# Hybrid attention layer on one core: value projection of two head pairs per product

## The chip, the cores and the metric

The kernel runs on 1 core of one Trainium2 chip. The time is device microseconds of one execution; runs are compared by their median. Three runs of the kernel before took 1176.5, 1177.23 and 1177.47 us, median 1177.23.

## The reference

One decoder layer on x (1 x 2048 x 1024, f32). A modulated RMS norm gives h, and one product gives all inputs of two attention branches:

```python
mod = jax.nn.silu(c) @ w_ada[l] + b_ada[l]
h = rms_norm(x, g_pre[l]) * (1.0 + scale[:, None, :]) + shift[:, None, :]
proj = h @ w_in[l]
qa, ka, va, fa, za, qb, kb, vb, zb = jnp.split(proj, split_points, axis=-1)
oa = forgetting_attention(qa, ka, va, fa + b_fgate[l]) * jax.nn.silu(za)     # 8 heads of 64, causal
ob = sliding_window_sink_attention(rope(qb), rope(kb), vb, sinks[l]) * jax.nn.silu(zb)   # 8 heads, window 128
y = jnp.concatenate([oa, ob], axis=-1) @ w_out[l]
x = x + gate[:, None, :] * rms_norm(y, g_post[l])
```

(Reshapes are left out.) The change concerns va = h @ w_in[:, 1024:1536], the values of the eight heads of the first ("fox") branch, and the order in which va and the gates zb of the second ("sliding window") branch are computed.

## The kernel before, in words

**Numbers in two parts.** To reach f32 accuracy with f16 products each matrix is kept as a high and a low f16 part, and a product is three matmuls: high x high, low x high, high x low. hT holds h transposed, in four chunks ("ci") of 512 positions, with 8 slices of the model dimension (KT = 8).

**Weights.** A weight tile of 128 columns goes through eight steps, each hung on a place of the work list: `w_load` (L211, a DMA issued by POOL into a raw tile, pool `wpool`, two buffers shared by all keys), `w_max` (L220, DVE), a round trip through DRAM (`w_back`), `w_scale` (L233, a chain of small DVE instructions), `w_high` (L251, one ACT instruction of 128 x 1024 at L256), two `w_low` (L259, DVE, L262) and `w_done`. The split parts are a tile tagged `whl`; it comes from `wpq` (one buffer) for keys that begin with q or k, else from `wpool` (two buffers). With one buffer, `w_high` of the next key waits until TensorE has read the last of the key before.

**The work list.** `punits` is a list of "units", each a piece of a projection that takes TensorE some 0.65 us: for z, q and k three matmuls of 512 columns (`proj_units`, L339), for the values twelve matmuls of 128 columns (`value_units`, L346 to L372, matmul at L357). A group of eight units holds one of three PSUM banks (`bk`), then ACT copies it out (L362), DVE makes the low part (L366, two instructions) and the bank is released. `add` (L940) appends units and hangs the weight steps on unit numbers ahead of the first use ("lead": load 42 units ahead, high 9 ahead). `after(n, f)` and `tick()` delay ACT and DVE pieces by ticks. Every engine executes its own instructions in the order in which this program emits them.

**The stages.** Up to unit 144 (some 148 us) h is built. Then, until unit 440 (some 416 us), 32 "windows" of sliding-window attention (`Pair`) are interleaved with units, about nine units to a window. A window on TensorE is `pv` (L924, 24 matmuls, tile pob), `turn` (L900, four transposes, tile pxb) and `scores` (L871, twelve matmuls, tile pss), some 2 us in all. Behind it come ACT `fold` (L905), DVE `fold` (L906), four POOL selects (L910, L912) that make `ptb`, which the next window's `pv` reads; and DVE `maxima` (L879 to L886, ends with `b_nb`), then four ACT exponentials (L893, tile sm_), which the next window's `turn` reads. So two chains run from one window to the next, one through ACT, DVE and POOL, one through DVE and ACT. After unit 440 come the first query/key projections and the rest of the values, then fox attention (scores from 477 to 1010 us), with the output projection from 975 us on.

**Order of groups before.** zb0, zb1, va0, zb2, zb3, va1, va2 among the windows (in the list at L962), va3 half before and half after the projection qk0 (L1026, L1060). Each va key is one pair of heads: 128 columns, four chunks of eight units.

**Scratch.** In the fox stage's last head and in the output stage a pool `stpo` (L1377) of four buffers of 2 KB per partition serves as raw storage of w_out and as scratch.

Of the kernel before, what the change touches and what calls it, by code (L numbers as in the profile page):

```python
# [10 lines left out]
F32 = mybir.dt.float32  # L11
F16 = mybir.dt.float16
BF16 = mybir.dt.bfloat16
# [22 lines left out]
XM, XR, VW = 66, 69, 129  # L36
# [7 lines left out]
def hybrid_layer(  # L44
# [17 lines left out]
    V, A, G, PE, SP = nc.vector, nc.scalar, nc.gpsimd, nc.tensor, nc.sync  # L62
# [64 lines left out]
    right = ExitStack()  # L127
# [16 lines left out]
    hT = [(hpool if i < 2 else hlate).tile([P, 2, KT, CH], F16, name=f"hT{i}") for i in range(NCH)]  # L144
# [33 lines left out]
    bk = [ps_bk.tile([P, CH], F32, name=f"bk{n}") for n in range(3)]  # L178
    held, order_ = set(), [0, 1, 2]

    def bank(hold=False):
        n = next(n for n in order_ if n not in held)
        order_.remove(n)
        order_.append(n)
        if hold:
            held.add(n)
        return n

    def release(n):
        held.discard(n)  # L190
        order_.remove(n)
        order_.append(n)
# [14 lines left out]
    wq = {}  # L207
# [43 lines left out]
    def w_high(key):  # L251
        raw, pw, sw = wq[key]
        width = VB if key == "vb" else P
        pool = vbw if key == "vb" else wpq if key[0] in "qk" else wpool
        whl = pool.tile([P, 2, KT, width], F16, tag="whl", name=f"wh_{key}")
        A.activation(whl[:, 0], raw[:], AF.Identity, scale=sw[:])  # L256
        wq[key].append(whl)

# [13 lines left out]
    def o_store(on, pool, ci, rows_, cols_, eng, lag):  # L272
# [11 lines left out]
        after(lag, lambda: A.activation(oh[:, :, 0], on, AF.Copy))  # L284
        after(lag + 1, low)

    pws = {}
    scl, isc, czs, kaps, nscl, snd = {}, {}, {}, {}, {}, {}

# [40 lines left out]
    def proj_units(key, ci, evac):  # L330

        st_ = {}

        def unit(k):
            if k == 0:
                st_[0] = bank(True)
            whl, ps = wq[key], bk[st_[0]][:]
            for n, (a, b) in enumerate(((0, 0), (0, 1), (1, 0))):
                PE.matmul(ps, whl[:, a, k, :], hT[ci][:, b, k, :],  # L339
                          start=(k == 0 and n == 0), stop=(k == KT - 1 and n == 2))  # L340
            if k == KT - 1:
                evac(ps, lambda: release(st_[0]))

        return [lambda k=k: unit(k) for k in range(KT)]

    def value_units(key, ci, dst):  # L346

        st_ = {}

        def unit(n_):  # L350
            if n_ == 0:
                st_[0] = bank(True)
            whl, ps = wq[key], bk[st_[0]][:]
            u = n_ // 2
            for k in range(4 * (n_ % 2), 4 * (n_ % 2) + 4):
                for n, (a, b) in enumerate(((0, 0), (1, 0), (0, 1))):
                    PE.matmul(ps[:, u * P:(u + 1) * P], hT[ci][:, a, k, u * P:(u + 1) * P], whl[:, b, k, :],  # L357
                              start=(k == 0 and n == 0), stop=(k == KT - 1 and n == 2))
            if n_ == 7:
                hi, lo = dst()  # L360
                pv4 = ps.rearrange("p (t h d) -> p t h d", t=4, h=2)
                after(1, lambda: A.activation(hi, pv4, AF.Copy, scale=PS_SCALE))  # L362

                def low():
                    for h in range(2):
                        V.scalar_tensor_tensor(lo[:, :, h], pv4[:, :, h], PS_SCALE, hi[:, :, h],  # L366
                                               op0=ALU.mult, op1=ALU.subtract)
                    release(st_[0])

                after(2, low)  # L370

        return [lambda n=n: unit(n) for n in range(8)]  # L372

    def evac_z(kt, key, ci):
        def evac(ps, free):
            t = op_.tile([P, CH], F32, tag="tz", name="tz")

            def mul():
                V.scalar_tensor_tensor(t[:], t[:], 1.0, ps, op0=ALU.add, op1=ALU.mult)
                free()  # L380
# [69 lines left out]
    start = ExitStack()  # L450
# [223 lines left out]
    fx, abp = {}, None  # L674

    def open_fox():
        nonlocal abp
        xlx.close()
        abp = swa_pool("abp", 4)
        early.close()  # L680
        fxv = right.enter_context(tc.tile_pool(name="fxv", bufs=1, side="right", reuse_waits="tile"))
        vt = fx["vt"] = fxv.tile([P, NB, 8, VW], F16, name="vt")
        fx["lk"] = fxv.tile([P, LW], F16, name="lk")
        fx["lq"] = [fxv.tile([P, LW], F16, name=f"lq{n}") for n in range(2)]
        fx["cst"] = cst = fxv.tile([P, XR], F16, name="cst")
# [12 lines left out]
    def va_units(j, ci):  # L698
        rows_ = slice(4 * ci, 4 * ci + 4)
        heads = slice(2 * j, 2 * j + 2)  # L700
        return value_units(f"va{j}", ci, lambda: (fx["vt"][:, rows_, heads, 0:64], fx["vt"][:, rows_, heads, 65:VW]))


    swa = ExitStack()

# [5 lines left out]
    stp = swa_pool("stp", 2)  # L711
# [7 lines left out]
    vb = kvp.tile([P, NB, 2, P], F16, name="vb")  # L719
# [218 lines left out]
    pkeys, punits = [], []  # L938

    def add(key, us):  # L940
        if key not in pkeys and key not in ("kb", "vb"):
# [24 lines left out]

    def at_slice(n, f):
        events.setdefault(n, []).append(f)
# [205 lines left out]
    foxl, foxo = ExitStack(), ExitStack()  # L1174
# [196 lines left out]
    def open_out():  # L1371
        nonlocal op_, stp
        foxl.close()
        hpx.close()
        wo = foxo.enter_context(tc.tile_pool(name="wo", bufs=1, reuse_waits="tile"))
        op_ = foxo.enter_context(tc.tile_pool(name="opo", bufs=2, reuse_waits="tile"))
        stp = foxo.enter_context(tc.tile_pool(name="stpo", bufs=4, reuse_waits="tile"))  # L1377
        oio["w"] = wo.tile([P, 2, KT, D], F16, name="wohl")

        fm = sm(1, "w_p2")  # L1380
        V.tensor_reduce(fm[:], fac8[:], axis=AX.X, op=ALU.max)
        V.reciprocal(fm[:], fm[:])
        V.tensor_tensor(ysc[:], wrt[:], fm[:], op=ALU.mult)
        V.tensor_scalar(wsc[:], fac8[:], ysc[:], None, op0=ALU.mult)
# [19 lines left out]
        V.scalar_tensor_tensor(w_slot(8 + k)[:, cc], raw[:], wsc[:, k:k + 1], hi, op0=ALU.mult, op1=ALU.subtract)  # L1404

    oio = {}

    class Out:

# [319 lines left out]
```

## Time and profile before

| what | us |
|---|---|
| median of 3 runs | 1177.23 |
| profiled execution | 1173.47 |
| its span, first to last instruction | 1171.7 |
| TensorE busy in the span | 1126.7 |
| VectorE (DVE) busy | 924.3 |
| ScalarE (ACT) busy | 661.7 |
| value matmuls of va (L357), busy, 1536 instructions | 91.9 |

The profiled execution is one run, with the hardware profiler on; 1.8 us of its time lie outside the span. "PE" is the matmul side of TensorE, "PEld" its weight loads, which overlap. In a row of a timeline the first number is the start in us from the start of the span, the second the time until the last of the merged instructions ended; in square brackets stands the idle time of the engine before it and what ended that. A matmul's shown duration holds its latency in the pipeline, so the pace of a stream of matmuls is read from start to start.

### The profile page before, as it was taken

To read this page: it belongs to the slowest core of one execution; us is meant where nothing else is said; L and a number is where in the kernel's file an instruction comes from. 1 tells how busy PE (TensorE), PEld (TensorE's weight loads), DVE (VectorE), ACT (ScalarE), POOL (GpSimd) and SP (SyncE) were. 2 spreads that over 40 slices of the span, in tenths; PEclk is the share of its full clock that TensorE was granted. 3 is DMA by queue.
4 is the path that set the end of the run, shared out by engine and by line. 5 is a ranking of instruction groups with operands and counts; after the bars stand their busy time and mean duration, and the time that the engine had idled before them with its cause. 6 is when DMAs were issued, how large, how long until landed. Compare 5 with 4: busy or idle time off the path is not lost.

```text
span 1171.7 us, 26770 instructions
## 1 busy us (share of the span) xinstructions
PE 1126.7 (96%) x10637; PEld 671.1 (57%) x10637; DVE 924.3 (79%) x2167; ACT 661.7 (56%) x1150; POOL 182.4 (16%) x293
## 2 busy tenths in 40 slices
PE   5899999999999999999999999999999999999997
PEld 2476555765558876555555555555556555544444
DVE  7876668677776548788888999888897897778885
ACT  2784445454555421476666767666676788633332
POOL 1000125535454421010000100001000000000000
PEclk9899999999999999999999999999999999999999
DMA  9745333314324323423424332222311237677742
GB/s 333 259 142 88 82 94 78 91 52 108 95 70 95 48 60 74 67 56 86 74 71 65 106 55 58 61 49 67 52 37 43 72 88 226 138 216 200 193 144 108
DMA packets 123481, 120.19 MB, mean 103 GB/s; under 512 B 64948, under 2 KB 100828, under 8 KB 123356
## 3 DMA queue, kind: packets, MB, share of 16 engines
q1 hardware_dynamic: 112088, 85.69, 27.1%
q0 software_dynamic: 10832, 32.50, 13.0%
q8 instruction: 83, 1.36, 0.6%
q14 instruction: 42, 0.34, 0.2%
q10 hardware_dynamic: 436, 0.28, 0.1%
HBM read 64.75 MB, written 25.18 MB: 77 GB/s over the span
## 4 chain that ended last, share of the span: by engine, by line
PE 74%; DVE 13%; DMA 7%; ACT 3%; issue 2%; SPq 1%; POOL 0%; DVEq 0%; ACTq 0%; POOLq 0%
PE bk L339 27%; PE bk L1522 13%; PE bk L357 7%; PE sta L1311 4%; PE sta L1310 4%; PE bk L1261 4%; PE poa L1336 3%; PE poa L1337 3%; PE poa L1334 3%; DMA wa<-in_w_ada_dram 2%; DVE a_m L1264 2%; PE pss L871 1%; PE pob L924 1%; DVE pha L1324 1%; PE pxb L900 1%
## 5 line engine op out<-in xcount | busy, mean ns | idle before, releaser
L1317 ACT ACTIVATE p<-sta,lift,scl_qk 128x1024 f32<-128x1024 f32 (+2 forms) x160 | 171.9, 1075 | 131.1 <-PE sta L1311 80.4
L339 PE MATMUL bk<-hT,wh_qk 128*128 128x512 f16 x768 | 194.7, 378 | 0.0
L1324 DVE TENSOR_TENSOR pha<-p,pha 128x1024 f16<-128x1024 f32 (+2 forms) x160 | 169.1, 1057 | 0.2 <-ACT pha L1321 0.2
L1264 DVE TENSOR_REDUCE a_m<-bk 128x1 f32<-128x512 f32 x192 | 130.4, 686 | 46.5 <-PE bk L1261 45.5
L1522 PE MATMUL bk<-wohl,oz 128*128 128x512 f16 x744 | 165.3, 379 | 1.0 <-DVE oz L1471 0.7
L1321 ACT ACTIVATE pha<-p 128x1024 f16<-128x1024 f32 (+2 forms) x160 | 148.1, 925 | 7.1 <-PE bk L1261 2.3
L1522 PEld LDWEIGHTS <-oz 128*128 128x128 f16 x744 | 71.9, 99 | 82.8 <-DVE oz L1471 1.8
L1337 PE MATMUL poa<-vt,pha 128*128 128x65 f16 x1088 | 116.0, 192 | 1.4 <-DVE pha L1324 1.4
L1334 PE MATMUL poa<-vt,pha 128*128 128x65 f16 x1088 | 116.6, 193 | 0.8 <-DVE ona L1343 0.7
L1336 PE MATMUL poa<-vt,pha 128*128 128x64 f16 x1088 | 116.6, 194 | 0.0
L339 PEld LDWEIGHTS <-wh_qk 128*128 128x128 f16 x768 | 72.2, 97 | 74.4 <-issue 1.9
L1310 PE MATMUL sta<-T 128*128 128x512 f16 (+1 forms) x320 | 110.9, 346 | 2.8 <-ACT p L1317 2.8
L1261 PE MATMUL bk<-T 66*128 66x512 f16 (+2 forms) x320 | 109.7, 348 | 2.5 <-DVE a_m L1264 1.9
L1334 PEld LDWEIGHTS <-pha 128*128 128x128 f16 x1088 | 101.5, 96 | 15.5 <-DVE ona L1343 1.9
L1311 PE MATMUL sta<-T 69*128 69x512 f16 (+1 forms) x320 | 109.8, 348 | 0.0
L1336 PEld LDWEIGHTS <-pha 128*128 128x128 f16 x1088 | 100.9, 97 | 11.4
L1337 PEld LDWEIGHTS <-pha 128*128 128x128 f16 x1088 | 100.8, 99 | 1.8 <-DVE pha L1324 1.8
L339 PE MATMUL bk<-hT,wh_za 128*128 128x512 f16 x384 | 99.7, 378 | 0.0
L357 PE MATMUL bk<-wh_va,hT 128*128 128x128 f16 x1536 | 91.9, 221 | 2.9 <-issue 2.8
L357 PEld LDWEIGHTS <-hT 128*128 128x128 f16 x1536 | 88.7, 99 | 7.4 <-issue 5.4
L339 PE MATMUL bk<-hT,wh_zb 128*128 128x512 f16 x384 | 88.9, 379 | 0.0
L339 PE MATMUL bk<-hT,wh_qb 128*128 128x512 f16 x384 | 87.6, 379 | 0.7 <-DVE wh_qb L262 0.7
(447 smaller groups left out, 1893.1 us busy)
## 6 DMA issues: line engine op xcount, KB each, us to landing
hT<-in_x_dram SPq DMA_DIRECT2D x20, 512.0 KB
wa<-in_w_ada_dram SPq DMA_DIRECT2D x16, 512.0 KB
z_d<-tz POOLq DMA_DIRECT2D x32, 256.0 KB
T<-stq SPq DMA_DIRECT2D x64, 128.0 KB
T<-z_d SPq DMA_DIRECT2D x16, 512.0 KB
out_dram<-hT SPq DMA_DIRECT2D x15, 512.0 KB
xt<-in_x_dram SPq DMA_DIRECT2D x12, 512.0 KB
qs<-qf SPq DMA_DIRECT2D x80, 64.0 KB
```

Of the source, the lines that this page charges most:

```text
L339: PE.matmul(ps, whl[:, a, k, :], hT[ci][:, b, k, :], start=(k == 0 and n == 0), stop=(k == KT - 1 and n == 2))
L357: PE.matmul(ps[:, u * P:(u + 1) * P], hT[ci][:, a, k, u * P:(u + 1) * P], whl[:, b, k, :], start=(k == 0 and n == 0), stop=(k == KT - 1 an ...
L1261: PE.matmul(mx[:, :w], T[0:XM, 0, i * P:(i + 1) * P], T[0:XM, 2, pc * CH:pc * CH + w], start=True, stop=True)
L1264: V.tensor_reduce(m3[:, u, pc:pc + 1], mx[:, :w], axis=AX.X, op=ALU.max)
L1310: PE.matmul(self.st[:, o:o + w], T[:, 3, kb_], T[:, 1, qc], start=True, stop=False)
L1311: PE.matmul(self.st[:, o:o + w], T[0:XR, 2, kb_], T[0:XR, 0, qc], start=False, stop=not diag)
L1317: A.activation(self.p32[:, :self.w], self.st[:, :self.w], AF.Exp, scale=scl[f"qk{self.hd}"][:], bias=lift[:])
L1324: V.tensor_tensor(self.ph[:, 1, :self.w], self.p32[:, :self.w], self.ph[:, 0, :self.w], op=ALU.subtract)
L1334: PE.matmul(po[:, u, :], ph[:, 0, pq], vt[:, b, hd, 0:65], start=(self.first and n == 0 and u == 0), stop=False)
L1336: PE.matmul(po[:, u, 0:64], ph[:, 0, pq], vt[:, b, hd, 65:VW], start=False, stop=False)
L1337: PE.matmul(po[:, u, :], ph[:, 1, pq], vt[:, b, hd, 0:65], start=False, stop=(self.last and n == len(self.blocks) - 1))
L1522: PE.matmul(py, self.hl[:, i, k, :], w_slot(8 * j + k)[:, cc], start=(k == 0 and m_ == 0), stop=(k == KT - 1 and m_ == 2))
```

## The change

The values of two pairs of heads are computed in one product of 256 columns: the weights of va0 and va1 lie side by side in one tile, those of va2 and va3 in a second one. Both tiles come from a new pool `wv` with one buffer and one tag. A unit is now six matmuls of 256 columns (two of the eight slices), and sixteen units make a chunk of a pair of pairs; eight units still fill one bank, which now holds two blocks of 128 positions for four heads. ACT's copy and DVE's two low parts handle as many elements as before. The matmuls of va fall from 1536 to 768, and so do their weight loads.

The order of groups becomes zb0, zb1, zb2, va0+va1 (units 256 to 360), zb3, va2+va3 (from unit 408). The weight steps of va0 are moved 40 units further ahead, those of va2 48 units, so that both halves of a tile are split one after the other. The steps of va2's `w_high` thus stand ahead of unit 351, those of va1 and va3 keep their leads. The pool `stpo` is replaced by quarters of a third tile of pool `wv`.

```diff
@@ w_high
-        whl = pool.tile([P, 2, KT, width], F16, tag="whl", name=f"wh_{key}")
+        if key[:2] == "va":
+            j = int(key[2:])
+            if j % 2 == 0:
+                wv[j // 2] = fx["wv"].tile([P, 2, KT, 2 * P], F16, tag="whl", name=f"wh_va{j}")
+            whl = wv[j // 2][:, :, :, (j % 2) * P:(j % 2 + 1) * P]
+        else:
+            whl = pool.tile([P, 2, KT, width], F16, tag="whl", name=f"wh_{key}")
@@ value_units
-    def value_units(key, ci, dst):
+    def value_units(p, ci, vt):
...
-            u = n_ // 2
-            for k in range(4 * (n_ % 2), 4 * (n_ % 2) + 4):
+            u, m = n_ // 4, n_ // 8
+            if n_ % 8 == 0:
+                st_[m] = bank(True)
+            ps = bk[st_[m]][:]
+            for k in range(2 * (n_ % 4), 2 * (n_ % 4) + 2):
                 for n, (a, b) in enumerate(((0, 0), (1, 0), (0, 1))):
-                    PE.matmul(ps[:, u * P:(u + 1) * P], hT[ci][:, a, k, u * P:(u + 1) * P], whl[:, b, k, :],
-                              start=(k == 0 and n == 0), stop=(k == KT - 1 and n == 2))
+                    PE.matmul(ps[:, (u % 2) * 2 * P:(u % 2 + 1) * 2 * P], hT[ci][:, a, k, u * P:(u + 1) * P],
+                              wv[p][:, b, k, :], start=(k == 0 and n == 0), stop=(k == KT - 1 and n == 2))
...
-        return [lambda n=n: unit(n) for n in range(8)]
+        return [lambda n=n: unit(n) for n in range(16)]
@@ open_fox
         vt = fx["vt"] = fxv.tile([P, NB, 8, VW], F16, name="vt")
+        fx["wv"] = right.enter_context(tc.tile_pool(name="wv", bufs=1, side="right", reuse_waits="tile"))
@@ add
+        if key in ("va01", "va23"):
+            for j in key[2:]:
+                add(f"va{j}", [])
+        elif key not in pkeys and key not in ("kb", "vb"):
...
+                if key in ("va0", "va2"):
+                    lead += {"va0": 40, "va2": 48}[key]
@@ order of groups
-    for kind, j in (("zb", 0), ("zb", 1), ("va", 0), ("zb", 2), ("zb", 3), ("va", 1), ("va", 2)):
+    for kind, j in (("zb", 0), ("zb", 1), ("zb", 2), ("va", 0), ("zb", 3), ("va", 1)):
         key = f"{kind}{j}"
-        others += [(key, va_units(j, ci) if kind == "va" else proj_units(key, ci, evac_z(4 + j, key, ci)))
-                   for ci in range(NCH)]
+        if kind == "va":
+            others += [(("va01", "va23")[j], us) for ci in range(4 - 2 * j) for us in va_units(j, ci)]
+        else:
+            others += [(key, proj_units(key, ci, evac_z(4 + j, key, ci))) for ci in range(NCH)]
...
-    for ci in range(2):
-        add("va3", va_units(3, ci))
+    for us in va_units(1, 2):
+        add("va23", us)
...
-    for ci in range(2, NCH):
-        add("va3", va_units(3, ci))
+    for us in va_units(1, 3):
+        add("va23", us)
@@ open_out
-        stp = foxo.enter_context(tc.tile_pool(name="stpo", bufs=4, reuse_waits="tile"))
+        stp = Quarters(fx["wv"].tile([P, 2, KT, 2 * P], F16, tag="whl", name="sv"))
```

`Quarters` is a new small class that hands out the four 2 KB quarters of that tile in turn.

More of the change, by code (lines that the diff above doesn't have):

```diff
@@ L285, in o_store @@
         after(lag + 1, low)
+    wv = {}
     pws = {}
@@ L344, in proj_units @@
         return [lambda k=k: unit(k) for k in range(KT)]
-    def value_units(key, ci, dst):
+    def value_units(p, ci, vt):
         st_ = {}
         def unit(n_):
-            if n_ == 0:
-                st_[0] = bank(True)
-            whl, ps = wq[key], bk[st_[0]][:]
-            u = n_ // 2
-            for k in range(4 * (n_ % 2), 4 * (n_ % 2) + 4):
-                for n, (a, b) in enumerate(((0, 0), (1, 0), (0, 1))):
-                    PE.matmul(ps[:, u * P:(u + 1) * P], hT[ci][:, a, k, u * P:(u + 1) * P], whl[:, b, k, :],
-                              start=(k == 0 and n == 0), stop=(k == KT - 1 and n == 2))
-            if n_ == 7:
-                hi, lo = dst()
-                pv4 = ps.rearrange("p (t h d) -> p t h d", t=4, h=2)
+            u, m = n_ // 4, n_ // 8
[3 more added lines that the diff above has]
+            for k in range(2 * (n_ % 4), 2 * (n_ % 4) + 2):
+                for n, (a, b) in enumerate(((0, 0), (1, 0), (0, 1))):
+                    PE.matmul(ps[:, (u % 2) * 2 * P:(u % 2 + 1) * 2 * P], hT[ci][:, a, k, u * P:(u + 1) * P],
+                              wv[p][:, b, k, :], start=(k == 0 and n == 0), stop=(k == KT - 1 and n == 2))
+            if n_ % 8 == 7:
+                t0, heads = 4 * ci + 2 * m, slice(4 * p, 4 * p + 4)
+                hi, lo = vt[:, t0:t0 + 2, heads, 0:64], vt[:, t0:t0 + 2, heads, 65:VW]
+                pv4 = ps.rearrange("p (t h d) -> p t h d", t=2, h=4)
                 after(1, lambda: A.activation(hi, pv4, AF.Copy, scale=PS_SCALE))
                 def low():
-                    for h in range(2):
-                        V.scalar_tensor_tensor(lo[:, :, h], pv4[:, :, h], PS_SCALE, hi[:, :, h],
+                    for t in range(2):
+                        V.scalar_tensor_tensor(lo[:, t], pv4[:, t], PS_SCALE, hi[:, t],
                                                op0=ALU.mult, op1=ALU.subtract)
-                    release(st_[0])
+                    release(st_[m])
                 after(2, low)
-        return [lambda n=n: unit(n) for n in range(8)]
+        return [lambda n=n: unit(n) for n in range(16)]
     def evac_z(kt, key, ci):
@@ L696, in const_turn, with va_units, va_group @@
         after(1, lambda: A.activation(fx["crow"][64:XR, :], px[64:XR, 0:P], AF.Copy))
[L698 to L701, printed above, removed]
+    def va_units(p, ci):
+        us = [lambda n=n: va_group(p, ci)[n]() for n in range(16)]
+        return us[:8], us[8:]
+    va_made = {}
+    def va_group(p, ci):
+        if (p, ci) not in va_made:
+            va_made[p, ci] = value_units(p, ci, fx["vt"])
+        return va_made[p, ci]
     swa = ExitStack()
@@ L940, in add @@
     def add(key, us):
-        if key not in pkeys and key not in ("kb", "vb"):
+        if key in ("va01", "va23"):
+            for j in key[2:]:
+                add(f"va{j}", [])
+        elif key not in pkeys and key not in ("kb", "vb"):
             at = len(punits) - {"za3": 4}.get(key, 20 if key[:2] == "za" else 0)
@@ L1406, in hybrid_layer, with __init__, tile @@
     oio = {}
+    class Quarters:
+        def __init__(self, whole):
+            self.flat, self.n = whole[:].rearrange("p a k n -> p (a k n)"), 0
+        def tile(self, shape, dtype, **kw):
+            v = self.flat[:, self.n * HALF:(self.n + 1) * HALF]
+            self.n = (self.n + 1) % 4
+            if dtype == F32:
+                return v.bitcast(F32)
+            if dtype == BF16:
+                v = v.bitcast(BF16)
+            return v.rearrange("p (a b) -> p a b", a=shape[1])
     class Out:
```

## The prediction

> **What bounds the kernel now.** I read the page first, then the list of groups, then the timeline of each engine from 290 to 430 us, where the values and the windows stand.
>
> ```profile
> span 1171.7 us, 26770 instructions
> ...
> PE 1126.7 (96%) x10637; PEld 671.1 (57%) x10637; DVE 924.3 (79%) x2167; ACT 661.7 (56%) x1150; POOL 182.4 (16%) x293
> ...
> PE 74%; DVE 13%; DMA 7%; ACT 3%; issue 2%; SPq 1%; POOL 0%; DVEq 0%; ACTq 0%; POOLq 0%
> ...
> L357 PE MATMUL bk<-wh_va,hT 128*128 128x128 f16 x1536 | 91.9, 221 | 2.9 <-issue 2.8
> L357 PEld LDWEIGHTS <-hT 128*128 128x128 f16 x1536 | 88.7, 99 | 7.4 <-issue 5.4
> ```
>
> TensorE is busy for 96% of the span and holds 74% of the chain that ended last. So in the stage of the values, time goes where TensorE gets shorter, or stops. ACT and DVE have room on average; they count only where one of them makes TensorE wait. The 91.9 us of the value matmuls are what the change touches.
>
> **The change part by part.**
>
> *1. Half as many value matmuls, twice as wide.* A stream of 128-column products, and one of 256 columns that the kernel has at its end:
>
> ```profile
> 416.96 10.88 PE L357 MATMUL bk<-wh_va,hT 128*128 128x128 f16 x192
> 427.68 0.86 PE L924 MATMUL pob<-vb,ptb 128*128 128x64 f16 x24
> ...
> 1158.50 5.40 PE L1486 MATMUL bk<-wohl,oz 128*128 128x256 f16 x48
> ...
> L1486 PE MATMUL bk<-wohl,oz x48: 272/272/273, 1158.5 to 1163.6; 128*128 128x256 f16 x48
> ```
>
> 192 products take 427.68 - 416.96 = 10.72 us, 55.8 ns each. The 48 wide ones take 5.40 us less the 0.27 us that a single one shows (272 ns), over 47 steps: 109 ns. A pair costs 111.6 now, then 109: 2.5 ns less. Times 768 that is **-1.9 us**. The weight loads are halved, but they lie under the matmuls (88.7 beside 91.9 us) and give nothing more. ACT's and DVE's copies move the same elements in the same number of instructions: nothing.
>
> *2. A new wait of ACT, at va2's high part.* The pool `wv` has one buffer. `w_high` of va2 stands ahead of unit 351, and va0+va1 is read until unit 359. In the built order of the changed kernel that ACT instruction waits for TensorE, and the copies out of both remaining va0+va1 groups behind it wait for nothing more: it waits for the last product of va0+va1. How long: rows for a window, for the ACT work and for the wait's release.
>
> ```profile
> 345.53 0.86 PE L924 MATMUL pob<-vb,ptb 128*128 128x64 f16 x24
> 346.23 0.64 PE L900 MATMUL pxb<-ident,sm__4807 128*128 128x128 f32 x4
> 346.80 0.67 PE L871 MATMUL pss<-kst,stb 64*128 64x128 f16 x12
> 347.40 1.47 PE L339 MATMUL bk<-hT,wh_qb 128*128 128x512 f16 x6
> 348.70 4.85 PE L357 MATMUL bk<-wh_va,hT 128*128 128x128 f16 x84
> ...
> 354.66 0.83 PE L871 MATMUL pss<-kst,stb 64*128 64x256 f16 x12
> 355.42 0.84 PE L357 MATMUL bk<-wh_va,hT 128*128 128x128 f16 x12
> 356.10 5.34 PE L339 MATMUL bk<-hT,wh_qb 128*128 128x512 f16 x24
> ...
> 338.44 0.60 ACT L905 ACTIVATE fold<-pxb 128x512 f16<-128x512 f32 x1 [1.71 <-PE pxb L900]
> ...
> 341.75 0.46 ACT L893 ACTIVATE sm__4807<-pss,b_nb,scl_qb 128x129 f32<-128x129 f32 x1 [2.41 <-DVE b_nb L886]
> ...
> 343.51 1.15 ACT L256 ACTIVATE wh_va<-wr_va,w_sw 128x1024 f16<-128x1024 f32 x1
> ...
> 356.30 0.60 ACT L362 ACTIVATE vt<-bk 128x512 f16<-128x512 f32 x1 [0.57 <-PE bk L357]
> ```
>
> From start to start: pob 0.70, pxb 0.57, pss 0.60 (first window of a head pair) or 0.76, six 512-wide products 1.30 us. The last value product before 356.10 lets ACT start at 356.30, 0.2 us after the next product began. ACT has finished its four exponentials 343.51 - 338.44 = 5.1 us after it began the fold, so some 5.2 us after pxb. From there TensorE, by the built order, still has 0.76 (pss) + 54 products of 256 columns (5.9) + 2.0 (next window) + 24 products (2.6) = 11.3 us from pxb to the last va0+va1 product. So ACT stands some **6 us**. What is queued behind it: two copies of va0+va1, the fold and the exponentials of the next window, w_high of zb3. DVE stands too, as its next instruction is va2's low part; behind that are the maxima. TensorE runs on until it needs what they owe. DVE's rows:
>
> ```profile
> 339.07 0.69 DVE L906 TENSOR_TENSOR fold<-pxb,fold 128x512 f16<-128x512 f32 x1 [0.73 <-ACT fold L905]
> ...
> 341.40 0.23 DVE L886 TENSOR_SCALAR b_nb<-b_m,nscl_qb 128x4 f32<-128x4 f32 x1
> ...
> 342.61 0.69 DVE L746 TENSOR_TENSOR qs<-qs,sinT 128x512 f32<-128x512 f32 x1
> ...
> 343.94 0.42 DVE L280 TENSOR_TENSOR oh<-on,oh 128x256 f16<-128x256 f32 x1
> 344.69 0.75 DVE L262 SCALAR_TENSOR_TENSOR wh_va<-wr_va,w_sw,wh_va 128x512 f16<-128x512 f32 x1 [0.33 <-ACT wh_va L256]
> 345.36 0.68 DVE L740 TENSOR_TENSOR stb<-qc,stb 128x512 f16<-128x512 f32 x1
> ...
> 347.35 0.41 DVE L930 TENSOR_TENSOR on<-pob,b_ri 128x256 f32<-128x256 f32 x1
> ...
> 359.38 0.75 DVE L366 SCALAR_TENSOR_TENSOR vt<-bk,vt 128x256 f16<-128x256 f32 x2
> ```
>
> Count from T, the end of the last va0+va1 product. ACT starts 0.2 us later, so va2's high part is there at 1.35. DVE: two low parts (0.67 each, 344.69 to 345.36) to 2.7, the value's low parts (0.7) to 3.4, `on` (0.33) to 3.75, then fold to b_nb (339.07 to 341.40: 2.33) to 6.1, b_nb done at 6.3. Four exponentials (1.76) end at 8.2, the last transpose at 8.4. TensorE without a wait: 18 products of qb3 (3.9), pob 0.70, pxb 0.57: 5.2. (Part of the stop comes earlier, at pob, since the POOL selects wait for DVE's fold; it is inside these numbers.) **First stop 3.2 us.** DVE then owes the next window: scale chain of zb3 1.2 (341.40 to 342.61), the two rope steps 1.33, oh 0.35, zb3's low half after ACT's 1.15 us for its high part (at 9.4 by then, 10.1 after), stb 0.6, value 0.7, the other half 0.67, two small ones 0.3, `on` 0.33, fold to b_nb 2.6 (a memset more), done at 15.5; exponentials to 17.4, transposes to 17.6. TensorE without a wait: 8.4 + 0.6 + 1.3 + 21 products of zb3 (4.5) + 1.27 = 16.1. **Second stop 1.5 us.** In the window after that TensorE has 27 products (5.8 us) and DVE little: no stop. Sum **+4.7 us**. Bounds: the exponentials have 346.23 - 343.51 = 2.7 us of slack in a window, so 6.0 - 2.7 = 3.3 us at the least; 6.0 us if nothing is made up. I take the walk, which lies between.
>
> *3. zb3 leaves the windows of qb3.* There the kernel stops now, since zb3 and qb3 are split in the same windows and qb3's high part waits for TensorE:
>
> ```profile
> 299.36 1.15 ACT L256 ACTIVATE wh_qb<-wr_qb,w_sw 128x1024 f16<-128x1024 f32 x1 [1.51 <-PE bk L339]
> ...
> 303.69 0.49 PE L924 MATMUL pob<-vb,ptb 128*128 128x64 f16 x5
> ...
> 306.18 0.83 PE L871 MATMUL pss<-kst,stb 64*128 64x256 f16 x12
> ```
>
> From 303.69, pob and pxb need 1.27, but pss starts at 306.18: 1.2 us lost. In the changed kernel qb3 is split alone there, and DVE has zb3's two halves (1.3 us) and its small instructions (0.3) less in front of the maxima, more than the stop: **-1.2 us**, between 0 (the 1.51 us wait stays and alone makes the stop) and 1.2. This row is also a small likeness of part 2: a wait of 1.5 us costs 1.2.
>
> *4. Loads and order.* va0's load, maximum and scale come beside zb2's; POOL's load of va0 waits for qb1's last low part, ahead of four selects that it needs only later. DVE gets up to 2.5 us more (a maximum and two halves) in two windows there; over that stage it has 34 us of 130 idle, some 2.1 in a window of 8:
>
> ```profile
> 200.00:330.00 130.00, 128.64 (x1345) 80.13 (x1344) 95.61 (x221) 68.11 (x219) 62.95 (x100) 1.00 0.33 83
> ```
>
> Nothing, from 0 to +1. va1 takes zb2's place beside qb2, with the same work. The scratch quarters keep the order of the instructions in the last stage: nothing.
>
> *5. A gap that may or may not belong to the change.* In the middle of va2, TensorE stands for 2.56 us with nothing in front of it, and then runs slowly:
>
> ```profile
> 388.06 4.19 PE L357 MATMUL bk<-wh_va,hT 128*128 128x128 f16 x72
> 394.81 3.71 PE L357 MATMUL bk<-wh_va,hT 128*128 128x128 f16 x36 [2.56 <-issue]
> 398.36 0.86 PE L924 MATMUL pob<-vb,ptb 128*128 128x64 f16 x24
> ...
> 394.95 0.60 ACT L362 ACTIVATE vt<-bk 128x512 f16<-128x512 f32 x1 [2.31 <-remote]
> ...
> 411.96 3.99 PE L357 MATMUL bk<-wh_va,hT 128*128 128x128 f16 x64 [0.21 <-issue]
> ...
> 396.00:397.00 1.00, 1.00 (x12) 1.00 (x10) 0.34 (x2) 0.00 (x0) 0.00 (x0) 0.50 1.05 242
> ...
> q8 instruction: 83, 1.36, 0.6%
> ```
>
> The 36 products take 3.55 us where 2.0 would do, at a granted clock of 0.50 (third column from the end of the window's row): gap and slow stretch are 4.1 us, with 0.2 at a second such place 4.3. If TensorE ran out of instructions there (its queue brings 16 KB pieces), half as many instructions would end it: -4.3. But ACT too stands until the same moment, and 192 products in a row from 416.96 see no such gap; so I take 0, and the other end is a rival. [...]
>
> **Sum:** -1.9 + 4.7 - 1.2 = **+1.6 us** on the profiled execution's 1173.47, so 1175.1. The median of the runs stands 3.76 us above that execution; I add the same 1.6 to it: 1177.23 + 1.6 = **1178.8 us**.
>
> **The rivals.**
>
> *A. The gap of part 5 goes with the narrow products.* For it: "issue" waits of TensorE's matmuls stand in L357 alone, where 36 instructions are used per us. Against: above. Time: 1178.8 - 4.3 = 1174.5.
>
> *B. Slower: the clock falls and a third window stops.* At T + 4 to T + 8.4 TensorE does little but pob and pxb; after the 2.56 us gap the clock was 0.50 and that cost 1.5. If it falls, and DVE's debt reaches a third window with another 1.5, the time is 1178.8 + 3.0 = 1181.8. [...] Against it: a slow TensorE after the first stop only eats the second, since that one is set by DVE. [...]
>
> *C. The wait costs little.* If ACT gets there later than 5.2 us after pxb, or DVE makes up the debt in the 3.9 us of qb3, only some 2 us are lost: 1178.8 - 2.7 = 1176.1. Against: DVE cannot start the maxima before the low parts.
>
> **How the numbers follow.** Forecast 0.42, A 0.30, B 0.18, C 0.10. About 0.2% (2.35 us) can be told from no change, so 1174.9 to 1179.6 is the same. Around each time I allow 1.5 us. Forecast: same 0.28, slower 0.14. A: faster 0.18, same 0.12. B: slower 0.17, same 0.01. C: same 0.06, faster 0.04. That is faster 0.22, same 0.47, slower 0.31; as part 3 and part 4 may each add or give about 1 us I round to 0.27, 0.43, 0.30. The range for 8 in 10 goes from just under A, 1173.4, to B, 1182.0.
>
> **What would show it.** Part 1: value products at 109 ns, some 84 us of them in all. Part 2: an ACT row of w_high with about 6 us of idle time released by TensorE, near 360 us, and in the next 20 us TensorE waiting for POOL (ptb) and ACT (sm_), 4.7 us together. Part 3: no wait near 304 us. Part 5: no issue gap in the values would speak for A, one of the same size for the forecast. The forecast is wrong if the stops behind the wait sum to under 3 or over 6 us, or if time goes in the fox stage, which I leave unchanged.

## The result: slower, 0.73% and not 0.13%

The changed kernel took 1184.43 us (median of 6, 1183.17 to 1187.84), the kernel before 1176.78 us beside it. The ratio is 1.0073, 95% interval 1.0057 to 1.0089. The forecast was 1178.8 us with a range up to 1182.0: the sign was right, the size was not, and the sum that gave it had two large errors of opposite sign. The profiled execution took 1183.17 us, against 1173.47 us before.

The page of the changed kernel, with the two value groups:

```profile
span 1181.4 us, 25231 instructions
...
PE 1132.2 (96%) x9869; PEld 662.3 (56%) x9869; DVE 925.8 (78%) x2167; ACT 660.6 (56%) x1150; POOL 182.4 (15%) x293
...
L364 PE MATMUL bk<-wh_va,hT 128*128 128x256 f16 x768 | 88.4, 273 | 0.0
L364 PEld LDWEIGHTS <-hT 128*128 128x128 f16 x768 | 74.2, 98 | 13.0 <-issue 2.1
```

TensorE is "busy" for 5.5 us more with 768 matmuls fewer. That column can't tell where the time is, because TensorE is shown as busy where it is slow, too: in the timeline below it is busy for all of the 2 us from 360, at a granted clock of 0.52, and four transposes are shown with 1.65 us that took 0.64 before. I read the stage by the starts of the scores (the row `pss`), one in each window, numbered from 0; they stand at the same places of the work list in every kernel here. The last column is the span.

| kernel | start of 0 | 4 to 13 | 18 to 19 | 22 to 25 | 29 to 30 | span |
|---|---|---|---|---|---|---|
| before | 148.11 | 74.39 | 9.09 | 24.24 | 12.32 | 1171.7 |
| after | 150.53 | 81.82 | 7.92 | 30.21 | 7.93 | 1181.4 |
| after, once more | 147.27 | 80.85 | 7.92 | 30.07 | 7.94 | 1175.4 |
| va2_later | 147.19 | 77.99 | 7.92 | 24.18 | 7.94 | 1167.6 |
| wsq_lag | 148.52 | 76.94 | 7.92 | 29.76 | 7.94 | 1172.6 |
| narrow | 146.80 | 79.16 | 8.02 | 36.42 | 8.07 | 1181.8 |
| no_trip | 149.08 | 74.22 | 7.92 | 29.79 | 7.93 | 1181.9 |
| order_only | 147.60 | 74.86 | 8.74 | 24.37 | 12.58 | 1173.9 |
| few_pieces | 144.33 | 74.71 | 7.91 | 30.06 | 7.94 | 1168.0 |
| few_later | 146.35 | 74.56 | 7.92 | 24.18 | 7.94 | 1163.3 |
| before_few | 146.75 | 74.39 | 8.94 | 24.23 | 8.06 | 1165.2 |
| narrow_few | 146.89 | 74.57 | 8.02 | 30.38 | 8.07 | 1170.9 |

The first two rows say it: **+7.4** us in windows 4 to 13 (part 4 of the prediction, "nothing"), **-1.2** at window 19 (part 3), **+6.0** in windows 22 to 25 (part 2, +4.7), **-4.4** at window 30 (the gap of part 5, "I take 0"), and 2.4 us ahead of the first window, where every engine's instructions stand in the same order in both kernels.

TensorE's timeline of the changed kernel at windows 24 and 25, then a row of ACT and one of DVE, and two windows' rows with the granted clock (third column from the end):

```profile
355.18 0.22 PE L938 MATMUL pob<-vb,ptb 128*128 128x64 f16 x2
356.39 0.26 PE L938 MATMUL pob<-vb,ptb 128*128 128x64 f16 x3 [0.99 <-POOL ptb L924]
356.97 0.73 PE L938 MATMUL pob<-vb,ptb 128*128 128x64 f16 x19 [0.33 <-POOL ptb L926]
358.19 1.65 PE L914 MATMUL pxb<-ident,sm__4725 128*128 128x128 f32 x4 [0.49 <-ACT sm__4725 L907]
359.77 0.91 PE L885 MATMUL pss<-kst,stb 64*128 64x128 f16 x12
360.61 2.74 PE L346 MATMUL bk<-hT,wh_qb 128*128 128x512 f16 x6
...
368.55 1.21 PE L914 MATMUL pxb<-ident,sm__4859 128*128 128x128 f32 x4
369.69 0.83 PE L885 MATMUL pss<-kst,stb 64*128 64x256 f16 x12
...
351.44 1.15 ACT L262 ACTIVATE wh_va<-wr_va,w_sw 128x1024 f16<-128x1024 f32 x1 [6.61 <-PE bk L364]
...
350.05 0.29 DVE L241 TENSOR_REDUCE w_mx<-mxr 128x1 f32<-128x128 f32 x1 [7.21 <-DMA mxr<-mx_d]
...
360.00:362.00 2.00, 2.00 (x16) 0.75 (x9) 1.70 (x4) 2.00 (x6) 0.78 (x1) 0.52 0.10 25
362.00:364.00 2.00, 2.00 (x8) 0.70 (x7) 1.97 (x5) 0.39 (x1) 1.53 (x2) 0.63 0.21 49
```

This is part 2 as it was walked through: ACT stands 6.61 us (some 6 were forecast) until the last product of va0+va1; then POOL's `ptb`, then ACT's exponentials are late. The four transposes take 1.65 us instead of 0.64: they start 0.44 us apart, as ACT's four exponentials do (357.59 to 358.91), and each waits for its own; PE's row has no bracket for that, the rows of its weight loads (PEld) have, 0.30 us ahead of each of the last three. One thing was not walked through: DVE stood too, for 7.21 us, for the broadcast of va2's own maximum, and made va2's scale only just ahead of ACT's start. By this trace alone either wait could have made the stop; the run `few_pieces` below tells them apart. Behind the stop the granted clock is 0.52, then 0.63 in the two rows (1.00 in every us from 354 to 360), a fall as rival B had it, and the six products that took 1.30 us take 2.54 (360.61 to the next row at 363.15).

The stage of part 4, by engine (PE, ACT, DVE, POOL, and SP's queue):

```profile
210.99 1.65 PE L914 MATMUL pxb<-ident,sm__2544 128*128 128x128 f32 x4 [0.47 <-ACT sm__2544 L907]
...
254.63 0.26 PE L938 MATMUL pob<-vb,ptb 128*128 128x64 f16 x3 [0.93 <-POOL ptb L924]
...
188.93 0.42 ACT L1163 ACTIVATE wsq<-wsq 128x256 f32<-128x256 f32 x1 [3.44 <-DMA wsq<-in_w_out_dram]
...
206.27 0.42 ACT L1163 ACTIVATE wsq<-wsq 128x256 f32<-128x256 f32 x1 [3.99 <-DMA wsq<-in_w_out_dram]
...
240.18 0.42 ACT L1163 ACTIVATE wsq<-wsq 128x256 f32<-128x256 f32 x1 [5.07 <-DMA wsq<-in_w_out_dram]
...
206.07 0.69 DVE L760 TENSOR_TENSOR qs<-qs,sinT 128x512 f32<-128x512 f32 x1 [3.18 <-DMA qs<-qf]
...
195.65 0.54 POOL L225 DMA_DIRECT2D mx_d<-w_mx  x1 [0.36 <-DVE w_mx L222]
...
239.68 0.54 POOL L230 DMA_DIRECT2D mxr<-mx_d  x1 [5.75 <-issue]
...
197.99 1.08 SPq L1167 DMA_DIRECT2D wsq<-in_w_out_dram  x2
...
mx_d<-w_mx POOLq DMA_DIRECT2D x1, 0.5 KB, 9.2
```

`mx_d<-w_mx` is the first leg of a weight's maximum: 128 numbers, one from each partition, to DRAM. That 0.5 KB transfer, issued at 195.65, lands 9.2 us later (last row, from the list of DMA issues), at 204.85. What was issued beside it lands when it does, or just behind: the rope's `qs` (DVE gets it at 206.07) and a 128 KB piece of w_out, `wsq`, issued at 197.99 (ACT gets it at 206.27). At 240.18 it looks the same with va1's maximum, issued at 229.44. ACT's fold, DVE's maxima and POOL's selects stand in order behind such waits.

### The profile page after: what moved, and what is told of

Same layout as the page of the kernel before. It is cut to its first block, busy times and chain, and to the rows that moved or that the text cites. A ratio compares the mean times of both kernels' runs of the same rounds, so it can differ in the third digit from the quotient of the medians.

```text
span 1181.4 us, 25231 instructions
## 1 busy us (share of the span) xinstructions
PE 1132.2 (96%) x9869; PEld 662.3 (56%) x9869; DVE 925.8 (78%) x2167; ACT 660.6 (56%) x1150; POOL 182.4 (15%) x293
## 3 DMA queue, kind: packets, MB, share of 16 engines
q8 instruction: 77, 1.26, 0.6%
## 5 line engine op out<-in xcount | busy, mean ns | idle before, releaser
L1355 PEld LDWEIGHTS <-pha 128*128 128x128 f16 x1088 | 101.5, 96 | 15.5 <-DVE ona L1364 1.9
L364 PE MATMUL bk<-wh_va,hT 128*128 128x256 f16 x768 | 88.4, 273 | 0.0
L364 PEld LDWEIGHTS <-hT 128*128 128x128 f16 x768 | 74.2, 98 | 13.0 <-issue 2.1
```

Source lines behind the costliest of these rows:

```text
L364: PE.matmul(ps[:, (u % 2) * 2 * P:(u % 2 + 1) * 2 * P], hT[ci][:, a, k, u * P:(u + 1) * P], wv[p][:, b, k, :], start=(k == 0 and n == 0), ...
L1355: PE.matmul(po[:, u, :], ph[:, 0, pq], vt[:, b, hd, 0:65], start=(self.first and n == 0 and u == 0), stop=False)
```

## The experiments

Theory 1: the maxima's small pieces hold up all transfers beside them; an additional weight prepared at that place, and zb2's stores, put late landings on the path (windows 4 to 13). Separately, ACT's wait for the one-buffer tile makes the stops at windows 23 to 25. Rivals: DVE simply has too many splits there; the order of groups costs; narrow products run out of instructions by themselves.

All are compared with the kernel before on the same chip; chips differ (1176.8 us on the first, 1172.2 to 1172.6 on these), so ratios are compared.

| run | median us | ratio to before | 95% interval |
|---|---|---|---|
| va2_later | 1168.97 | 0.9983 | 0.9969 to 0.9998 |
| wsq_lag | 1177.79 | 1.0051 | 1.0031 to 1.0071 |
| before_wsq_lag | 1171.92 | 1.0002 | 0.9989 to 1.0014 |
| narrow | 1184.07 | 1.0106 | 1.0088 to 1.0125 |
| after once more | 1177.10 | 1.0042 | 1.0029 to 1.0055 |
| no_trip | 1181.76 | 1.0077 | 1.0063 to 1.0091 |
| before_no_trip | 1171.14 | 0.9991 | 0.9982 to 0.9999 |
| order_only | 1174.19 | 1.0019 | 1.0008 to 1.0030 |
| few_pieces | 1170.22 | 0.9976 | 0.9965 to 0.9987 |
| before_few | 1166.79 | 0.9946 | 0.9932 to 0.9959 |
| few_later | 1165.07 | 0.9935 | 0.9923 to 0.9947 |
| narrow_few | 1172.93 | 1.0000 | 0.9992 to 1.0009 |

### The reference once more

> The changed kernel itself once more, as the reference for the other three of this call, and to see which of its losses come back. From the ratio on record (1.0073) about 1180.8 us where the kernel before takes 1172.2. By the theory of late landings the stops at 358 to 372 us (6.0 us) and those at 246 to 268 us (some 3 us) are there each time, while those at 194 and 211 us (3.2 us in the first profile) come and go with the landing times, and so does the 2.4 us ahead of the first window.

The ratio is 1.0042, 4.9 us. What comes back is in the table: 80.85 us in windows 4 to 13, 30.07 in 22 to 25. So did the stop at 211 us, which was expected to come and go (9.58 us for that window in this run). What doesn't come back is the 2.4 us ahead of the first window and most of the stop behind ACT's 188.93 row (that window takes 8.47 us instead of 9.23, where 7.86 is free of waits). So 1.0073 holds some 3.7 us that this measurement, on another chip, does not; whether the run or the chip makes them was not shown.

### ACT's wait at va2's high part

```diff
-                    lead += {"va0": 40, "va2": 48}[key]
+                    lead += {"va0": 40, "va2": 30}[key]
```

> The changed kernel with one number changed: the weight steps of va2 are 30 units further ahead instead of 48, so that va2's high part (now ahead of unit 369) no longer has to wait for the last product of va0+va1 (unit 359). Theory 1 (ACT's wait at the one-buffer tile makes the stops at 358 to 372 us): the two stops and the half-clock stretch behind them, 6.0 us by the starts of the windows in the profile, go; median 1184.4 - 5.5 = about 1179, from 1178 to 1180. Theory 2 (three weight splits in a row on DVE make them, whoever waits): the splits are still three in some 25 units, and only about 2 us go: 1182.5.

TensorE's timeline at window 24:

```profile
347.24 0.86 PE L938 MATMUL pob<-vb,ptb 128*128 128x64 f16 x24
347.94 0.63 PE L914 MATMUL pxb<-ident,sm__4710 128*128 128x128 f32 x4
348.50 0.67 PE L885 MATMUL pss<-kst,stb 64*128 64x128 f16 x12
```

No wait is left there: 24.18 us from window 22 to 25, as before the change, 5.9 us less than in "after, once more" (30.07). The medians differ by 0.59%, 6.9 us; windows 4 to 13, where this edit changes nothing, took 2.9 us less too (77.99), so not all of the 6.9 is its work. On one chip and with few pieces the same edit gives 5.2 us (`few_pieces` and `few_later` below). Theory 1 for this part: it is the wait, not the number of splits.

### ACT's wait for w_out's pieces

```diff
-            if n:
-                A.activation(wsq[n - 1][:], wsq[n - 1][:], AF.Square, ...)
+            if n > 1:
+                A.activation(wsq[n - 2][:], wsq[n - 2][:], AF.Square, ...)
...
```

> The changed kernel, but ACT's sum of squares of a piece of w_out (wsq) is taken one window later, so that ACT, whose fold stands behind it, no longer waits for a piece that lands late. Theory 1 (7.4 us between the fourth and the thirteenth window are lost because the maxima's round trip of 4-byte pieces holds up whatever is issued beside it, and ACT, DVE and POOL stand behind such transfers in turn; ACT for 12.5 us at wsq): ACT's share goes, DVE's wait for its rope step at 206 us stays; 2 to 4 us less, median 1180.4 to 1182.4. Theory 2 (DVE's three weight splits between 200 and 260 us are what is late): nothing, 1183.9 to 1184.9, and the stops at 194, 211, 246 and 256 us stay.

> The kernel before with the same edit (squares of w_out one window later), to see what the edit gives where few pieces land late: ACT's waits for wsq sum to 1.8 us in its profile. Theory 1 and theory 2 alike: 0 to 0.7 us less than the kernel before, 1176.1 to 1176.8. If it gains 2 us or more here too, the edit helps for another reason than the late landings of the changed kernel.

ACT's wait went, and what that gave stays open. By the medians it is between nothing (1.0051 against 1.0042 in "after, once more") and 2.6 us (against 1.0073), each on another chip. The profile, of the fastest of six runs that spread over 6.9 us, has 76.94 us in windows 4 to 13, 3.9 less than "after, once more"; but va2_later, where nothing was changed in these windows, had 77.99. What stayed is the stop ahead of window 12's scores. Three engines stood for the same cause, and with ACT's wait gone the others still stand. POOL, DVE and PE of wsq_lag, and the landing of the broadcast `mxr` of that window:

```profile
232.50 0.54 POOL L230 DMA_DIRECT2D mxr<-mx_d  x1 [5.04 <-issue]
...
234.00 2.12 DVE L900 TENSOR_SCALAR b_nb<-b_m,nscl_qb 128x4 f32<-128x4 f32 x1
236.12 0.29 DVE L241 TENSOR_REDUCE w_mx<-mxr 128x1 f32<-128x128 f32 x1
...
246.86 0.26 PE L938 MATMUL pob<-vb,ptb 128*128 128x64 f16 x3 [0.93 <-POOL ptb L924]
...
DMA to landing us min/median/max: 10.2/10.2/10.2
```

qb2's broadcast, issued at 225.9, lands 10.2 us later, at 236.1. DVE's `b_nb`, otherwise 0.2 us long, has ended only when the instruction that needs the broadcast starts (why, the row doesn't say); all that DVE owes is late from there, and TensorE stops at 246.86 as in the changed kernel (254.63; 10.72 us for that window in both). My share for ACT was not confirmed; the cause stayed open between late landings and DVE's splits. The kernel before gained nothing, as expected.

### The maxima's trip left out; the order alone

In no_trip the four keys' `w_max` sends nothing and `w_scale` uses each partition's own maximum. order_only changes one list of the kernel before:

```diff
-(("zb", 0), ("zb", 1), ("va", 0), ("zb", 2), ("zb", 3), ("va", 1), ("va", 2))
+(("zb", 0), ("zb", 1), ("zb", 2), ("va", 0), ("va", 1), ("zb", 3), ("va", 2))
```

> The changed kernel with a part of the computation left out: for the keys zb2, va0, qb2 and va1 the maximum over the partitions is not taken, so that their round trip through DRAM (128 pieces of 4 bytes out, a broadcast of 64 KB back) is gone; each row of these weights is scaled by its own maximum. All loads, splits, products and copies stay. Theory 1 (late landings: the small pieces hold up the rope's and w_out's transfers, and the broadcast, for which DVE and POOL wait in order): the stage from the fourth to the thirteenth window gets as short as in the kernel before or shorter, 3.5 to 7 us less than the changed kernel, about 1175 to 1177. Theory 2 (DVE's splits are simply too many there): only what DVE's reductions took, under 1 us.

> The kernel before with the same part left out for the keys that it prepares in that stage (va0, qb2, zb2). Theory 1: its windows 11 to 13 have a stop of about 2 us too (DVE 2.6 us longer in the twelfth and thirteenth window); 1 to 2.5 us less than the kernel before. Theory 2: under 0.7 us less.

> The kernel before with only its groups in the changed order (zb0, zb1, zb2, va0, va1, zb3, va2, and va3 as before), 128 columns per product, each key's weight steps at its own lead, no shared tile. It tells the order apart from the width and from the early steps of va0 and va2. Theory 1: va0 isn't prepared beside zb2, so the stage of windows 4 to 13 is as before within 1 us; zb3's stop at 304 us goes (-1.2); the gap at 392 us depends on where a round trip falls, so it stays (0) or goes (-4.4): 1171 if it stays, 1167 if it goes. Theory 2 (the order alone costs, as zb2's copies and stores stand where va0's copies stood): 3 us more than before, 1175.

Windows 4 to 13 take 74.22 us without the trips, 6.6 less than with them, and 74.86 with the order alone. So neither DVE's splits nor the order cost anything worth naming there: the trips do. But no_trip as a whole is slower (1.0077). It loses more behind the windows: some 7 us from the last window's scores to the first fox scores, and 4.7 us from there to the end. The largest piece has the same look: one of q's and k's transfers comes just behind another key's maximum, which was issued at 443.66 and landed 13.2 us later, at 456.9:

```profile
457.09 0.61 PE L1287 MATMUL bk<-T 66*128 66x512 f16 x1 [5.66 <-DMA T<-stq]
```

In before_no_trip the stop at window 13, for which theory 1 wanted 1 to 2.5 us, shrank by 0.3 us only (9.80 to 9.46 us for that window); every kernel here has that stop, and its cause was not tested. order_only lost 2.2 us by its ratio, in other windows: its gap stayed (12.58), zb3's stop shrank by 0.35 only, and windows 13 to 18, where it prepares va1 beside qb3, take 42.37 us instead of 39.63. That was not followed up.

### 4 pieces instead of 128

```diff
...
-        V.tensor_reduce(mx[:], wq[key][0][:], axis=AX.XY, op=ALU.max, apply_absolute_value=True)
+        V.tensor_reduce(mx[:, 0:1], wq[key][0][:], axis=AX.XY, op=ALU.max, apply_absolute_value=True)
+        V.transpose(mt[:], mx[:])
...
-        G.dma_start(md[:], mx[:])
+        G.dma_start(md.rearrange("(a b) o -> a (b o)", a=4), mt[0:P:32, :])
```

All work is kept, so this is the cleanest test (mx is 128 x 32 here, zero beyond its first column).

> The changed kernel, all of its work kept, but each key's 128 maxima leave as 4 pieces of 128 bytes instead of 128 pieces of 4 bytes: DVE first transposes them in blocks of 32 x 32 (one more instruction per key). Theory 1 (the small pieces hold up every transfer beside them): the maxima land some 2 to 3 us after issue instead of 9, the stops between the fourth and the thirteenth window go, the two stops at 351 to 365 us (va2's high part) stay: 6.5 us less than the changed kernel, ratio to the kernel before 1.0042 - 0.0055 = 0.9987. Theory 2 (it is the broadcast back, 128 times 512 bytes, or the stores of z beside it): the landings stay at some 9 us and the time changes by under 1 us.

> The kernel before with the same transposed maxima. Theory 1: its gap of 2.56 us at 392 us with the half clock behind it (4.4 us by the starts of the windows) goes too, since TensorE's instructions come through the same DMA engines as the pieces that hold them up, and of the 2.6 us at windows 12 and 13 some 2 go: 5 to 7 us less than the kernel before, ratio 0.9945 to 0.9955. Theory 2 (the gap is TensorE's own rate of instructions): the gap stays, under 2 us less.

> Both edits on the changed kernel: transposed maxima, and va2's steps 30 units ahead instead of 48. If the two causes (late landings, ACT's wait at the tile with one buffer) add up, 6.5 + 5.8 us less than the changed kernel: ratio to the kernel before 0.994 to 0.9935. If they overlap, less.

The maxima's time to landing in the changed kernel (the profile tells it for 4 of the 23), in the changed kernel once more (for 8) and in few_pieces (for all 23):

```profile
DMA to landing us min/median/max: 8.8/9.1/10.2
```

```profile
DMA to landing us min/median/max: 6.6/8.2/9.5
```

```profile
DMA to landing us min/median/max: 1.6/1.7/3.9
```

The broadcast back, 64 KB and not changed, took 6.2 to 9.2 us in the changed kernel (2 landings told) and 3.1 to 5.0 in few_pieces. ACT's waits for w_out in the changed kernel (few_pieces has none), and ACT's wait for TensorE at va2's high part in few_pieces:

```profile
  DMA wsq<-in_w_out_dram: 12.5, 3
```

```profile
338.26 1.15 ACT L268 ACTIVATE wh_va<-wr_va,w_sw 128x1024 f16<-128x1024 f32 x1 [6.18 <-PE bk L370]
```

before_few has its gap gone (4.3 us) and 1.4 us ahead of the first window, and nothing of the 2 us that theory 1 wanted at windows 12 and 13.

In the changed kernel windows 4 to 13 fall from 80.85 to 74.71 us. All five profiles of the new order with the old pieces have 76.9 to 81.8 us there, the three with few pieces 74.6 to 74.7. The ratio, 0.9976, is lower than the 0.9987 expected. The stops of part 2 stay (30.06), though va2's broadcast is no longer late; so it is the tile with one buffer that makes them, and they go when va2 is later (few_later, 24.18). The two causes add up: 1.0042, 0.9976 and 0.9935. few_later beats both kernels; against before_few (0.9946) the intervals overlap, so that the change is then worth something is likely and not shown.

### The gap, and the width

```diff
-            for k in range(2 * (n_ % 4), 2 * (n_ % 4) + 2):
+            c = n_ % 4 // 2
+            for k in range(4 * (n_ % 2), 4 * (n_ % 2) + 4):
...
-                    PE.matmul(ps[:, (u % 2) * 2 * P:(u % 2 + 1) * 2 * P], ..., wv[p][:, b, k, :], ...)
+                    PE.matmul(ps[:, (u % 2 * 2 + c) * P:(u % 2 * 2 + c + 1) * P], ..., wv[p][:, b, k, c * P:(c + 1) * P], ...)
```

> The changed kernel with all value products 128 columns wide again (1536 matmuls and weight loads), in the same order of groups, from the same tiles. Theory 1 (a pair of narrow products costs 2.5 us per thousand more than a wide one): 1.9 us more, median 1186.3. Theory 2 (the gap of 2.56 us and the half clock behind it, in the narrow values at 392 us of the kernel before, come from TensorE running out of instructions, which need twice the rate): such a gap stands in the profile again and the time is 4 us above that, about 1190; without a gap theory 2 falls or the gap needs a coincidence.

> The changed kernel with transposed maxima and products of 128 columns, to have the price of the width without gaps. Theory 1: no gap; 768 pairs at 2.5 ns are 1.9 us over the same kernel with 256 columns, ratio 1.0003. Theory 2 (narrow products run out of instructions whatever the DMAs do): a gap as in the narrow kernel before this one (7.2 us between two windows), ratio 1.004 or more.

The narrow kernel, TensorE and ACT at windows 22 to 23, with two windows' rows (the last two columns are the busy share of the DMA engines, which adds up the times of packets and so can exceed 1, and the GB/s that they moved):

```profile
337.47 0.42 PE L365 MATMUL bk<-wh_va,hT 128*128 128x128 f16 x2 [2.10 <-issue]
339.31 7.56 PE L365 MATMUL bk<-wh_va,hT 128*128 128x128 f16 x88 [1.42 <-issue]
...
337.67 0.60 ACT L920 ACTIVATE fold<-pxb 128x512 f16<-128x512 f32 x1 [5.29 <-remote]
...
334.00:336.00 2.00, 1.38 (x24) 1.06 (x19) 0.00 (x0) 0.00 (x0) 0.00 (x0) 1.00 1.28 12
336.00:338.00 2.00, 0.42 (x2) 0.14 (x2) 0.00 (x0) 0.33 (x1) 0.00 (x0) 0.86 0.19 2
```

A gap like that of part 5, at another place: two weights' maxima were issued ahead of it, at 322.26 and 324.91, the DMA engines move 2 to 12 GB/s, and PE, ACT, DVE and POOL all stand. When the second maximum landed, the profile doesn't tell; a store of 128 KB issued between the two took 14.1 us, until 337.9. The kernel before with few pieces, where its gap was (windows 29 and 30):

```profile
385.99 6.20 PE L363 MATMUL bk<-wh_va,hT 128*128 128x128 f16 x108
392.03 0.86 PE L930 MATMUL pob<-vb,ptb 128*128 128x64 f16 x24
```

No gap: 8.06 us instead of 12.32. With wide products there is none with the old pieces either: windows 22 to 25 take 30.07 us in "after, once more" and 36.42 in the narrow kernel, which has the same order and the same transfers, and 30.38 with narrow products and few pieces. So there the gap needs both, small pieces and twice the matmuls per us (one in 55.8 ns instead of one in 109); each edit alone removes it. That it is instructions that do not arrive fits this, and that ACT stands too; no row names it. Among the DMA queues of the page, `q8 instruction` has 83 packets (1.36 MB) before and 77 (1.26 MB) in the changed kernel, with 768 matmuls and as many weight loads fewer, so TensorE's instructions come by that queue; that one of its packets, come late, makes the gap was not shown.

Without gaps, narrow_few is 0.24% slower than few_pieces, 2.7 us (some 1.7 either way by the intervals); 1.9 were forecast.

## Why the prediction was wrong, point by point

- **Part 1, -1.9 us: right.** A stream of wide products runs at 109 ns as forecast: 54 of them, from 402.46 to 408.36, take 5.90 us.

```profile
402.46 6.07 PE L364 MATMUL bk<-wh_va,hT 128*128 128x256 f16 x54
408.36 0.86 PE L938 MATMUL pob<-vb,ptb 128*128 128x64 f16 x24
```

- **Part 2, +4.7 us: the mechanism was right, the size some 1 us too small.** Windows 22 to 25 took 5.8 and 6.0 us more, near the upper bound of 3.3 to 6.0. Counted from T (351.24, the start of the product behind the last of va0+va1), the walk had the transposes of the first stop done at 8.4, and the scores behind them start at 359.77, 8.5 after T. The second stop was to end at 17.6 and ended at 18.45 (369.69): the step that failed is the sum of what DVE owes in the second window, 0.85 too small. `b_nb` was done at 16.2 and not at 15.5, and some 0.5 of that is zb3's second low half, which took 1.17 us where 0.67 was counted (rows below). POOL's select beside it took 1.08 instead of 0.63; why both were slow, no row shows. The rest stands ahead of the wait, at window 23 (up to 0.5). The clock fell as rival B had it (0.50 in every half us from 360.5 to 363.0; after how long an idle time it falls, no run shows), and as the argument against that rival said it only ate into the second stop, since the transposes there still waited for ACT (1.21 us for four); no third stop came.

```profile
362.47 1.17 DVE L268 SCALAR_TENSOR_TENSOR wh_zb<-wr_zb,w_sw,wh_zb 128x512 f16<-128x512 f32 x1
...
367.18 0.23 DVE L900 TENSOR_SCALAR b_nb<-b_m,nscl_qb 128x4 f32<-128x4 f32 x1
...
363.05 1.08 POOL L926 TENSOR_SCALAR_AFFINE_SELECT ptb<-fold 128x512 f16<-128x512 f16 x1
```

- **Part 3, -1.2 us: right** (9.09 to 7.92). The stop of the kernel before was zb3 and qb3 in the same windows.
- **Part 4, "nothing, from 0 to +1": wrong, and the step that failed.** It cost 7.4 and 6.5 us in the two profiles of the changed kernel, and 3.6 in va2_later's, where nothing was changed in these windows. I weighed the moved steps by DVE's free time and named the wait of POOL's load, and that would have been right: without the small pieces the stage is 0.2 to 0.3 us longer than before. I did not count the maximum's round trip as a transfer with a duration of its own, nor ask what was issued beside it. That was the term put at nothing: the maxima took 7 to 10 us each to land, and what stood behind them in order came late. The list of waits of the kernel before had it (us in total, times, longest):

```profile
POOL mxr L230 <- DMA mx_d<-w_mx: 64.3, 16, 7.6
```

- **Part 5, 0: wrong by 4.4 us the other way.** The gap went, as rival A said, but not by the narrow products alone: the narrow kernel, with 1536 of them in the new order, has none in windows 29 and 30 either (8.07). In the new order no maximum is on its way there: the changed kernel issues them at 374.47 and 414.74, the kernel before at 385.12, 7 us ahead of its gap. What the wide products spare is a new gap between windows 22 and 23, where the narrow kernel has one. The counter-argument, that 192 narrow products in a row show no gap, failed because it compared a stretch without a maximum on its way with one that had one.
- **The sum.** -1.9 + 5.8 - 1.2 + 6.5 - 4.4 = +4.8 us is what the second measurement found (+4.9). The first, 8.6 by its ratio, has some 3.7 us more; how much of that is the chip and how much the run stays open.
- **The fox stage** was left out of the change, rightly: from its first scores (`sta`, 477.5 before and 487.1 after) to the end of the span it takes 694.2 and 694.3 us. (In the four kernels with few pieces it takes 695.4 or 695.5; why, was not followed up.)

## What to carry to other kernels

A step that is moved brings its DMAs, and a small DMA can be a long one (0.5 KB took up to 10.2 us here): look up the time to landing of each, and what other queues issue in that time, before calling a move free. Where several in-order engines wait behind the same late transfer, taking one engine's wait away can show little, as the others still stand (between nothing and 2.6 us here); change the transfer (80.85 to 74.71 us in windows 4 to 13). And the gaps with no releaser that stood on several engines at once went here when the maxima left in fewer pieces (12.32 to 8.06 us, 36.42 to 30.38), so ask what the DMA engines do at such a gap, and not only the engine that shows it.

## What the runs showed of the hardware

- 128 pieces of 4 bytes (0.5 KB) took 8.8 to 10.2 us to land in one profile of the changed kernel and 6.6 to 9.5 in the other, and transfers issued beside them were late too: SP's `qs` and `wsq` let DVE and ACT go on at 206.07 and 206.27, just behind a maximum that landed at 204.85, and a store `z_d`, issued by POOL at 202.38, took 7.4 us where the median of its kind is 3.2. As 4 pieces of 128 bytes the same numbers took 1.6 to 3.9 us, and ACT's waits for `wsq` were gone. Why such pieces take so long, no row shows.
- The granted clock was 0.50 in every half us from 360.5 to 363.0, with 0.57 and 0.52 in the half us ahead and behind and 1.00 from 354 to 360 and from 363.5 to 366 (the 0.52 and 0.63 shown above are means of 2 us). It fell after a stretch in which TensorE was shown as busy for 0.99 and 1.47 of 2 us and no single wait in brackets reached 1 us:

```profile
356.00:358.00 2.00, 0.99 (x22) 0.75 (x22) 1.83 (x7) 0.41 (x2) 0.92 (x2) 1.00 0.00 0
358.00:360.00 2.00, 1.47 (x12) 0.78 (x14) 1.90 (x7) 2.00 (x9) 0.00 (x0) 1.00 0.00 0
```
